# One weight sum of every seven-product unit moved from VectorE to GpSimd, in a two-layer decoder trunk

## The chip, the cores and the metric

The kernel runs on one core of a Trainium2 chip. The metric is the device time of one execution in microseconds (us). All matrices are float32, held as pairs of a rounded part and a rest.

## The reference

Two layers, each with a half-step feed-forward network (FFN) before and after a mixer; layer 0 mixes with retention, layer 1 with gated linear attention (GLA). 16 learned tokens are put ahead of the 512, so 528 tokens with 1024 features run through:

```
for i in range(2):
    h = h + 0.5 * swiglu(rmsnorm(h, norm_ffn1[i]), ffn1_w_in[i], ffn1_w_out[i])   # 1024 -> 2 x 2816 -> 1024
    hn = rmsnorm(h, norm_mix[i])
    h = h + (retention(hn, ...) if i == 0 else gla(hn, ...))
    h = h + 0.5 * swiglu(rmsnorm(h, norm_ffn2[i]), ffn2_w_in[i], ffn2_w_out[i])
h = rmsnorm(h, final_norm)
return h[:, 16:]
```

Nearly all of the time goes into the projections: the input and output matrices of the four FFNs (called f10, f20, f11, f21 in tile names, in the order f10, retention, f20, f11, GLA, f21) and of the two mixers.

## The kernel before

**Units of seven products.** Most weight matrices are used in units: two blocks of 128 weight columns against 528 tokens in two halves of 264, done by the Strassen-Winograd scheme with seven block products in place of eight. A unit's weight has the quarters a11, a12, a21, a22, each 128 rows by 512 (384 in the middle group of an FFN's output matrix). The products need four sums of them as well: s1 from a22 and a21, s3 from a11 and a21, s2 from s1 and a11, s4 from a12 and s2. `Weights.order` gives the order of the seven: UNIT (a11, s1, s2, a12, s4, s3, a22), LAST (s3 and s4 swapped), PARTED (a11, s1, a12, s2, ...), and FIRST (s1, s2, a12, a11, ...). PARTED is used in the first output unit of the last group of f10, f20 and f11; FIRST in the first unit of each FFN. Of the 150 units, 146 begin with a11 and 4 with s1.

**How a sum comes about.** SP loads a22 and a11 into a tile `pair` (two halves; L149), and then GpSimd issues one DMA that reads a21 and adds it to both (L155); after that the pair holds s1 and s3. There are three pair tiles, so a pair is loaded when the third unit before it has had its s3 or s1 split. Other quarters go into seven tiles `raw` (L158). VectorE makes s2 in the tile of a11 (L195: `raw<-pair,raw`) and later s4 in the tile of a12 (L197: `raw<-raw,raw`).

**Splitting.** `Weights._split` takes the plan's next weight: ScalarE rounds it into `whi` (L188), VectorE takes the rest into `wlo` (L189, weight minus `whi`). Seven pairs of those tiles are in the pool; the splits run some items ahead of the products (AHEAD = 4). A product is three matmuls per 128 x 128 block: hi with hi (L488), rest of the tokens (L489), rest of the weight (L490).

**Results.** A unit has a PSUM bank X, used several times, and a double bank QZ. ScalarE copies products out of X and Z (L727, L729, L734 to the tiles `su`, `szf` and others), and VectorE adds them (L1035, L998, L1070, L1077 among others). The next product that goes to X waits for that copy or addition, so these are the places where TensorE can come to wait for the two.

**What sets the order.** A scheduler puts each engine's instructions into one fixed order when the program is built; each engine then takes its own in that order and waits at the head of its queue for the semaphores of what it needs. That holds for the DMA issues too: an L155 on GpSimd's queue waits until its two SP loads have landed, and what stands behind it on that queue waits with it.

Of the kernel before, what the change touches and what calls it, by code (L numbers as in the profile page):

```python
# [68 lines left out]
class Weights:  # L69
# [92 lines left out]
    def _split(self, upto):  # L162
        V = self.nc.vector
        while self.split < min(upto, len(self.plan)):
            i = self.split
            home = next(((pool, there) for pool, n, there in self.homes if len(there) < n), None)
            if not home:
                break
            home[1].add(i)
            _, c, q, n, order = self.plan[i]  # L170
            self._load()
            if order:

                late = order[0] == "s1"
                s2 = self.tiles[c][:, 1] if late else self.tiles[c, "a11"]
                raw = {"s1": self.tiles[c][:, 1], "s3": self.tiles[c][:, 0], "s2": s2,
                       "s4": self.tiles[c, "a12"]}.get(q)
            if not order or raw is None:
                raw = self.tiles[c, q]
            hi = home[0].tile([P, PW], F32R, tag="hi", name=f"whi{i}")  # L180
            lo = home[0].tile([P, PW], F32R, tag="lo", name=f"wlo{i}")
            with ExitStack() as order_:
                if self.behind and i < self.FRONT:
                    for ins in self.behind:
                        order_.enter_context(self.tc.issue_after(ins.ins))
                if self.after:
                    order_.enter_context(self.tc.issue_after(self.after.ins))
                act = self.nc.scalar.copy(hi[:, :n], raw)  # L188
                dve = V.tensor_sub(lo[:, :n], raw, hi[:, :n].bitcast(F32))  # L189
                self.newest = act, dve  # L190
            self.parts[i] = (hi, lo)
            self.split += 1
            if order:
                if q == ("s1" if late else "a11"):
                    V.tensor_add(s2, self.tiles[c][:, 1], self.tiles[c, "a11"])  # L195
                elif q == "a12":
                    V.tensor_add(raw, raw, s2)  # L197
                self.over["pair"] += q == "s3"
                self.over["raw"] += q in self.OVER[2 if order == self.PARTED else late]
            else:  # L200
                self.over["raw"] += 1
            self._load()
# [2146 lines left out]
```

## Time and profile before

| | |
|---|---|
| median of 3 runs (lowest, highest) | 2019.59 us (2019.57, 2020.69) |
| profiled execution | 2020.17 us, of which the span of instructions 2018.4 us |
| TensorE busy | 1998.6 us, 99% of the span |
| VectorE busy | 1793.7 us, 89% |
| ScalarE busy | 1190.6 us, 59% |
| GpSimd busy | 209.8 us, 10%, in 181 instructions |
| granted TensorE clock | 0.999 |

All times in rows are microseconds from the start of the span. In a timeline row stand start, duration, engine (PE TensorE, DVE VectorE, ACT ScalarE, POOL GpSimd, SP the load queue), the line of the kernel, the operation with output and inputs, and in brackets the idle time before it with what ended it. TensorE's matmuls overlap in the rows (each is listed with 0.28 us and the next starts 0.12 us later), so its busy time says that it was never long without work, not more. A DVE row of 0.69 us starts some 0.60 us before the next when both stand back to back.

### The profile page before, as it was taken

To read this page: it belongs to the slowest core of one execution; us is meant where nothing else is said; L and a number is where in the kernel's file an instruction comes from. 1 tells how busy PE (TensorE), PEld (TensorE's weight loads), DVE (VectorE), ACT (ScalarE), POOL (GpSimd) and SP (SyncE) were. 2 spreads that over 40 slices of the span, in tenths; PEclk is the share of its full clock that TensorE was granted. 3 is DMA by queue.
4 is the path that set the end of the run, shared out by engine and by line. 5 is a ranking of instruction groups with operands and counts; after the bars stand their busy time and mean duration, and the time that the engine had idled before them with its cause. 6 is when DMAs were issued, how large, how long until landed. Compare 5 with 4: busy or idle time off the path is not lost.

```text
span 2018.4 us, 43487 instructions
## 1 busy us (share of the span) xinstructions
PE 1998.6 (99%) x16576; PEld 1964.3 (97%) x16576; DVE 1793.7 (89%) x3302; ACT 1190.6 (59%) x2427; POOL 209.8 (10%) x181
## 2 busy tenths in 40 slices
PE   9999999999999999999999999999999999999998
PEld 9999999999999999999999999999999989999998
DVE  8999999978787889989999998999897868999896
ACT  5756566555555465656666665666745544666664
POOL 1011111010101000111111011111001000211110
PEclk9999999999999999999999999999999999999999
DMA  7586877364545432776875477777525441687772
GB/s 228 138 208 168 205 194 188 101 163 121 157 132 147 132 116 74 181 202 161 213 186 163 128 189 187 180 199 181 183 69 126 105 137 65 159 208 182 185 191 69
DMA packets 176113, 318.87 MB, mean 158 GB/s; under 512 B 17568, under 2 KB 40736, under 8 KB 175904
## 3 DMA queue, kind: packets, MB, share of 16 engines
q1 hardware_dynamic: 133856, 237.04, 35.8%
q0 software_dynamic: 40896, 75.51, 23.4%
q10 hardware_dynamic: 1152, 3.55, 0.6%
q8 instruction: 130, 2.13, 0.4%
q14 instruction: 79, 0.65, 0.1%
HBM read 311.76 MB, written 4.26 MB: 157 GB/s over the span
## 4 chain that ended last, share of the span: by engine, by line
PE 83%; DVE 12%; ACT 2%; issue 2%; DMA 1%; POOL 0%; POOLq 0%; DVEq 0%; ACTq 0%
DVE wlo L189 4%; PE po_r L488 1%; PE po_r L489 1%; PE po_r L490 1%; PE lv L1866 1%; ACT whi L188 1%; DVE hf L521 1%; PE Xf21o L488 1%; PE Xf21o L490 1%; PE Xf21o L489 1%; PE Xf20u L488 1%; PE Xf11u L488 1%; PE Xf20u L490 1%; PE Xf11u L490 1%; PE Xf11u L489 1%
## 5 line engine op out<-in xcount | busy, mean ns | idle before, releaser
L188 ACT CAST whi<-raw 128x512 fp32r<-128x512 f32 (+1 forms) x893 | 531.9, 606 | 424.6 <-DVE raw L197 145.9
L189 DVE TENSOR_TENSOR wlo<-raw,whi 128x512 fp32r<-128x512 f32 (+1 forms) x893 | 590.3, 669 | 104.6 <-ACT whi L188 91.4
L188 ACT CAST whi<-pair 128x512 fp32r<-128x512 f32 (+1 forms) x304 | 183.4, 604 | 75.1 <-DVE pair L195 12.4
L189 DVE TENSOR_TENSOR wlo<-pair,whi 128x512 fp32r<-128x512 f32 (+1 forms) x304 | 201.8, 665 | 11.7 <-ACT whi L188 10.6
L155 POOL DMA_DIRECT2D pair<-in_f_in x73 | 89.0, 1220 | 704.6 <-DVE wlo L189 348.0
L197 DVE TENSOR_TENSOR raw<-raw,raw 128x512 f32<-128x512 f32 (+1 forms) x146 | 97.5, 668 | 3.6
L195 DVE TENSOR_TENSOR raw<-pair,raw 128x512 f32<-128x512 f32 (+1 forms) x146 | 97.2, 666 | 3.4 <-DMA pair<-in_f_in 0.8
L155 POOL DMA_DIRECT2D pair<-in_f_out x44 | 53.5, 1216 | 358.3 <-DVE wlo L189 122.8
L488 PE MATMUL po_r<-ogh,whi 128*128 128x264 f32 x256 | 71.7, 280 | 0.1
L489 PE MATMUL po_r<-ogl,whi 128*128 128x264 f32 x256 | 71.5, 279 | 0.0
L490 PE MATMUL po_r<-ogh,wlo 128*128 128x264 f32 x256 | 71.2, 278 | 0.0
L155 POOL DMA_DIRECT2D pair<-in_ret_in x20 | 24.4, 1222 | 308.6 <-DVE wlo L189 156.3
L999 ACT ACTIVATE gf<-gf 128x528 f32<-128x528 f32 (+1 forms) x36 | 23.2, 644 | 50.4 <-DVE gf L998 50.3
L488 PE MATMUL Xf11o<-hf,whi 128*128 128x264 f32 x176 | 49.5, 281 | 1.4 <-ACT szf L734 0.4
L488 PE MATMUL Xf20o<-hf,whi 128*128 128x264 f32 x176 | 49.5, 281 | 1.4 <-DVE x L1077 0.6
L488 PE MATMUL Xf10o<-hf,whi 128*128 128x264 f32 x176 | 49.5, 281 | 1.0 <-ACT szf L734 0.4
L489 PE MATMUL Xf11o<-hf,whi 128*128 128x264 f32 x176 | 49.1, 279 | 0.0
L489 PE MATMUL Xf20o<-hf,whi 128*128 128x264 f32 x176 | 49.1, 279 | 0.0
L489 PE MATMUL Xf10o<-hf,whi 128*128 128x264 f32 x176 | 49.1, 279 | 0.0
L488 PEld LDWEIGHTS po_r<-ogh,whi 128*128 128x128 f32 x256 | 48.0, 188 | 0.9 <-ACT k L521 0.3
L490 PE MATMUL Xf20o<-hf,wlo 128*128 128x264 f32 x176 | 48.9, 279 | 0.0
L490 PE MATMUL Xf10o<-hf,wlo 128*128 128x264 f32 x176 | 48.9, 279 | 0.0
(1183 smaller groups left out, 8598.8 us busy)
## 6 DMA issues: line engine op xcount, KB each, us to landing
raw<-in_f_in SPq DMA_DIRECT2D x277, 256.0 KB, 3.7
pair<-in_f_in SPq DMA_DIRECT2D x150, 256.0 KB, 5.0
pair<-in_f_in POOLq DMA_DIRECT2D x73, 512.0 KB, 7.4
raw<-in_f_out SPq DMA_DIRECT2D x80, 256.0 KB, 3.3
raw<-in_ret_in SPq DMA_DIRECT2D x76, 256.0 KB, 3.0
raw<-in_f_out SPq DMA_DIRECT2D x72, 192.0 KB, 3.0
pair<-in_f_out SPq DMA_DIRECT2D x48, 256.0 KB, 4.9
pair<-in_f_out POOLq DMA_DIRECT2D x24, 512.0 KB, 6.1
```

What stands on the lines that cost most here:

```text
L155: nc.gpsimd.dma_start(t, aps[2].unsqueeze(1).broadcast_to([P, 2, n]), accum_op=ALU.add)
L188: act = self.nc.scalar.copy(hi[:, :n], raw)
L189: dve = V.tensor_sub(lo[:, :n], raw, hi[:, :n].bitcast(F32))
L195: V.tensor_add(s2, self.tiles[c][:, 1], self.tiles[c, "a11"])
L197: V.tensor_add(raw, raw, s2)
L488: nc.tensor.matmul(ps, lhsT=lh, rhs=rh, start=start, stop=False, **kw)
L489: nc.tensor.matmul(ps, lhsT=lh, rhs=rl, start=False, stop=False, **kw)
L490: return nc.tensor.matmul(ps, lhsT=ll, rhs=rh, start=False, stop=stop, **kw)
L521: return S.copy(hi, src), V.tensor_sub(lo, src, hi.bitcast(F32))
L999: S.activation(o, o, AF.Silu, scale=-1.0)
L1866: nc.tensor.matmul(ps[:, j, J * P:J * P + n], lhsT=Kt[:, j, J * P:(J + 1) * P], rhs=q, start=(J == 0), stop=(J == 3), skip_group_check=True)
```

## The change

In units that begin with a11, the instruction L195, s2 = s1 + a11, is issued on GpSimd in place of VectorE. In the four units that begin with s1 it stays. s4 and all splits stay where they are.

```
             if order:
                 if q == ("s1" if late else "a11"):
-                    V.tensor_add(s2, self.tiles[c][:, 1], self.tiles[c, "a11"])
+                    (V if late else self.nc.gpsimd).tensor_add(s2, self.tiles[c][:, 1], self.tiles[c, "a11"])
                 elif q == "a12":
                     V.tensor_add(raw, raw, s2)
```

The scheduler then places 146 additions on GpSimd's queue between its DMA issues. On GpSimd, at the end of f10, the difference reads as follows (numbers behind a name count buffers: `pair36` and `raw94` belong to the first output unit of the last group, a PARTED one, and `pair38` to the second unit behind it):

```order
 L155 DMA pair36_4010<-in_f1_out 128x2x512
+L195 TENSOR_TENSOR raw91_3930<-pair35_3863,raw91_3930 128x512
 L155 DMA pair37_4148<-in_f1_out 128x2x512
 L155 DMA pair38_4276<-in_f1_out 128x2x512
+L195 TENSOR_TENSOR raw94_4065<-pair36_4010,raw94_4065 128x512
 L155 DMA pair39_4455<-in_f1_out 128x2x512
```

The sum of unit 36 stands behind the accumulating DMA of unit 38, that of unit 37 (not shown) behind the DMA of unit 39. On VectorE the same place reads as follows:

```order
+L197 TENSOR_TENSOR raw92_3972<-raw92_3972,raw91_3930 128x512
 L189 TENSOR_TENSOR wlo195_4273<-pair35_3863,whi195_4272 128x512
 L1003 TENSOR_TENSOR gf1021_4089<-Xf10g20_4090,su3_4092 128x264
-L197 TENSOR_TENSOR raw92_3972<-raw92_3972,raw91_3930 128x512
 L189 TENSOR_TENSOR wlo196_4294<-raw92_3972,whi196_4293 128x512
 L189 TENSOR_TENSOR wlo197_4313<-raw93_3991,whi197_4312 128x512
 L189 TENSOR_TENSOR wlo198_4332<-raw94_4065,whi198_4331 128x512
-L195 TENSOR_TENSOR raw94_4065<-pair36_4010,raw94_4065 128x512
 L189 TENSOR_TENSOR wlo199_4349<-pair36_4010,whi199_4348 128x512
 L189 TENSOR_TENSOR wlo200_4368<-raw95_4110,whi200_4367 128x512
```

Two things moved: L197 of the unit before now stands ahead of `wlo195`, the split that frees the pair tile for `pair38`; and the addition leaves the queue with nothing in its place. L197 of this unit (`raw95<-raw95,raw94`), L189 of `raw94` and then L1035 still follow in that order, and L197 now waits for GpSimd. On ScalarE, in retention, the rows around the split of a sum are these in the program of the change, the same as before but for what the second row waits for (`raw200` is the sum, made on GpSimd behind the DMA of `pair90`):

```order
L1432 COPY vt31_9470<-Xrv30_9471 128x264
L188 CAST whi394_9710<-raw200_9304 128x512
L734 COPY su5_9588<-Xrv32_9586 128x264
L188 CAST whi395_9727<-raw201_9428 128x512
L188 CAST whi396_9962<-pair78_9140 128x512
```

The copy L734 out of the bank `Xrv32`, behind it on the queue, moves with the cast.

More of the change, by code (lines that the diff above doesn't have):

```diff
@@ L194, in _split @@
                 if q == ("s1" if late else "a11"):
-                    V.tensor_add(s2, self.tiles[c][:, 1], self.tiles[c, "a11"])
+                    (V if late else self.nc.gpsimd).tensor_add(s2, self.tiles[c][:, 1], self.tiles[c, "a11"])
                 elif q == "a12":
```

## The prediction

> **What bounds the kernel now.** I read the page's shares first, then busy time by stretch, then the chain of waits, then single places in the timeline.
>
> ```profile
> PE 1998.6 (99%) x16576; PEld 1964.3 (97%) x16576; DVE 1793.7 (89%) x3302; ACT 1190.6 (59%) x2427; POOL 209.8 (10%) x181
> PE 83%; DVE 12%; ACT 2%; issue 2%; DMA 1%; POOL 0%; POOLq 0%; DVEq 0%; ACTq 0%
> ...
> L195 DVE TENSOR_TENSOR raw<-pair,raw 128x512 f32<-128x512 f32 (+1 forms) x146 | 97.2, 666 | 3.4 <-DMA pair<-in_f_in 0.8 <-DVE wlo L189 0.6
> ...
> 205.00:300.00 95.00, 95.00 (x813) 94.97 (x812) 87.81 (x158) 60.56 (x128) 13.39 (x11) 1.00 0.81 204
> 1050.00:1130.00 80.00, 78.79 (x658) 77.36 (x657) 76.52 (x140) 48.50 (x94) 6.79 (x6) 1.00 0.50 136
> ```
>
> The reader sees a kernel bound by TensorE: of 2018.4 us it lacks work for 19.8, and inside an FFN (205 to 300 us) for none, while VectorE there is at 87.81 of 95 us (92%). Only where one stage hands over to the next (1050 to 1130 us) is VectorE at 96% and TensorE short of work by 1.2 us. So 97.2 us of VectorE's work can go away and save almost nothing; what counts is whether something that TensorE waits for comes later. The chain's 12% of VectorE says where it is close. In the chain's pieces in order of time the instruction that moves appears ten times, the first and the last being
>
> ```profile
> 72.56 0.69 DVE raw L195
> ...
> 1784.94 0.70 DVE raw L195
> ```
>
> **What the change removes.** 146 additions of 0.666 us leave VectorE: 97.2 us of its busy time. On the path lie ten of them, 6.8 us at most, and that only if nothing takes their place. Inside the FFNs TensorE hides them, and would hide them still.
>
> **What the change adds: the price of a sum on GpSimd.** No row shows a GpSimd addition of 512 columns. The nearest rows are its small power operations, in the table of GpSimd's groups and in two stretches of the timeline:
>
> ```profile
> L462 POOL TENSOR_TENSOR rc<-ms_n,rc 128x1 f32<-128x1 f32 x4 | 2.2, 549 | 0.0
> ...
> 1535.82 1.03 POOL L462 TENSOR_TENSOR r_go<-ms_go,rc 128x4 f32<-128x4 f32 x1 [3.91 <-DVE ms_go L541]
> ...
> 1520.99 0.69 DVE L189 TENSOR_TENSOR wlo<-raw,whi 128x512 fp32r<-128x512 f32 x1
> 1521.16 1.40 POOL L462 TENSOR_TENSOR r_go<-ms_go,rc 128x4 f32<-128x4 f32 x1 [7.68 <-DVE ms_go L541]
> ```
>
> One column takes 0.55 us and four take 1.03, so a column of powers costs 0.16 and the fixed part is 0.55 - 0.16 = 0.39. The same four columns took 1.40 us when VectorE was 0.17 us into a subtraction of two SBUF tiles: 0.37 more. The streaming of 512 columns I take from VectorE, whose back-to-back rows start 0.61 us apart (296.86 and 297.47 below). My estimate is 0.39 + 0.61 + 0.37 = 1.37 us. The floor is 0.55 (the one-column operation); the top is 0.39 + 2 x 0.67 + 0.61 = 2.34, for half VectorE's rate behind a whole VectorE instruction. I take 1.37 because VectorE is at work nearly always, as in the 1.40 row. [...]
>
> **Where the price is hidden.** Most sums are free to start early: GpSimd's last DMA issue is long over, and the cast that reads the sum is late for other reasons. A unit in f10:
>
> ```profile
> 245.28 1.21 POOL L155 DMA_DIRECT2D pair<-in_f_in  x1 [7.00 <-DVE su L1036]
> 246.97 0.69 DVE L195 TENSOR_TENSOR raw<-pair,raw 128x512 f32<-128x512 f32 x1
> 250.22 1.14 ACT L188 CAST whi<-raw 128x512 fp32r<-128x512 f32 x2
> ```
>
> GpSimd is free at 246.49, the sum could end at 248.3, and its cast came at 250.22. With 1.37 us and each sum put behind its predecessor on the new queue, 130 of the 146 delay nothing that TensorE waits for by more than 0.05 us.
>
> **Where it is not hidden.** In 30 units the DMA issue that now stands ahead of the sum ended after the sum had begun on VectorE. That DMA can't come sooner: it waits for two loads, and these for the last split of an earlier pair. I list three kinds.
>
> First, the PARTED unit at the end of f10, f20 and f11, where L197 needs the sum almost at once:
>
> ```profile
> 296.86 0.69 DVE L195 TENSOR_TENSOR raw<-pair,raw 128x512 f32<-128x512 f32 x1
> 297.47 0.69 DVE L189 TENSOR_TENSOR wlo<-pair,whi 128x512 fp32r<-128x512 f32 x1
> 298.31 1.21 POOL L155 DMA_DIRECT2D pair<-in_f_out  x1 [6.62 <-DVE wlo L189]
> 298.84 0.69 DVE L197 TENSOR_TENSOR raw<-raw,raw 128x512 f32<-128x512 f32 x1
> 300.33 0.43 DVE L1035 TENSOR_TENSOR su<-Xf10u,su 128x264 f32<-128x264 f32 x1
> 301.53 0.28 PE L488 MATMUL Xf10u<-thf,whi 128*128 128x264 f32 x1
> ...
> 1044.76 0.69 DVE L197 TENSOR_TENSOR raw<-raw,raw 128x512 f32<-128x512 f32 x1
> 1045.43 1.22 POOL L155 DMA_DIRECT2D pair<-in_f_out  x1 [7.25 <-DMA pair<-in_f_out]
> ...
> 1380.10 0.69 DVE L197 TENSOR_TENSOR raw<-raw,raw 128x512 f32<-128x512 f32 x1
> 1380.58 1.22 POOL L155 DMA_DIRECT2D pair<-in_f_out  x1 [6.92 <-DVE wlo L189]
> ```
>
> At 297 us the DMA ends at 299.52, the sum at 300.89, and L197 starts 2.05 us later than at 298.84. L197 and one split at 0.61 each ended at 300.06, so VectorE had 0.27 us to spare before L1035; the matmul at 301.53, which needs L1035, had 0.77 (301.53 - 300.76). TensorE waits 2.05 - 0.27 - 0.77 = 1.0 us. The same at 1044.76 (DMA ends 1046.65, L197 3.26 late) gives 2.2, at 1380.10 (1381.80, 3.07 late) 2.0: together 5.2. The order adds 0.6 to each, since L197 of the unit before now stands ahead of the split that frees the pair: 1.8 more.
>
> Second, the unit after each of these. Here ScalarE stands still: the cast waits for the sum, and the copy out of X is queued behind the cast.
>
> ```profile
> 308.80 1.22 POOL L155 DMA_DIRECT2D pair<-in_f_out  x1 [9.27 <-DVE x L1076]
> 309.50 0.62 ACT L188 CAST whi<-raw 128x512 fp32r<-128x512 f32 x1 [0.33 <-DVE raw L195]
> 310.02 0.37 ACT L734 COPY szf<-Xf10o 128x264 f32<-128x264 f32 x1
> 310.94 0.28 PE L488 MATMUL Xf10o<-hf,whi 128*128 128x264 f32 x1
> ```
>
> The sum would end at 310.02 + 1.37 = 311.39, the cast start 1.9 us late, the copy with it; the matmul had 0.55 to spare: 1.4. In the other two FFNs the picture is the same: 4.2 in all.
>
> Third, retention and GLA, with the same queue on ScalarE and less to spare:
>
> ```profile
> 487.22 1.22 POOL L155 DMA_DIRECT2D pair<-in_ret_in  x1 [8.34 <-DVE raw L195]
> 487.47 0.62 ACT L188 CAST whi<-raw 128x512 fp32r<-128x512 f32 x1 [0.95 <-PE Xrv L489]
> 489.40 0.37 ACT L734 COPY su<-Xrv 128x264 f32<-128x264 f32 x1
> 490.14 0.28 PE L488 MATMUL Xrv<-rth,whi 128*128 128x264 f32 x1
> ...
> 689.08 0.62 ACT L188 CAST whi<-raw 128x512 fp32r<-128x512 f32 x1 [0.50 <-DVE wlo L189]
> 689.32 1.22 POOL L155 DMA_DIRECT2D pair<-in_f_in  x1 [7.88 <-DVE wlo L189]
> 689.60 0.37 ACT L734 COPY su<-Xrv 128x264 f32<-128x264 f32 x1
> 690.35 0.28 PE L488 MATMUL Xrv<-rth,whi 128*128 128x264 f32 x1
> ```
>
> At 689 us the sum ends at 691.91, the cast is 2.83 late, and the matmul after the copy had 0.38: 2.45. At 487 us the cast is 2.34 late, 0.5 of that is made up before the copy, and 0.37 is to spare: 1.4. Four more places, at 413, 495, 613 and 1546 us, are worth 2.4 by the same steps. Inside the FFNs (229, 1310, 1785 and 1862 us) there are 1.5.
>
> **The sum.** 5.2 + 1.8 + 4.2 + 2.45 + 1.4 + 2.4 + 1.5 = 19 us. Against it stands what VectorE gains on the path, between 0 and 6.8; I take 2, since eight of the ten pieces lie at hand-overs that now wait for the sum. That is 2020.2 + 17 = 2037 us. The profiled execution lies 0.6 above the median shown; I leave that in. With a sum of 0.55 us the same places give 7, with 2.34 some 43.
>
> **Rivals.** *Half of it* (2027): a wait hides a later one, for once TensorE stands still at 301.5 everything that it needs next has been given that much more time. For this speaks that the second kind follows the first by 10 us; against it, that the DMA of the second kind is itself freed by VectorE, which is late too. It holds if the cast of the second kind is no later against TensorE than before: 19 - 4.2 - 1.8 - 2 = 11, less what ScalarE makes up in retention, leaves 7.
>
> *VectorE held up* (2050): GpSimd's read stops VectorE's two-input instructions for its whole length, as the 1.40 row shows the other way round. Then each sum costs VectorE up to 1.37 - 0.39 = 0.98 us in place of 0.61; net 146 x 0.37 = 54 us, and at the 20 or so units near hand-overs, where VectorE is as full as at 1050 to 1130 us, it goes straight on: 7 us, and the waits of the sum grow by about as much, as more of the sums come late. Against it: inside the FFNs 7 us in 95 are free. [...]
>
> *Faster* (2014): GpSimd's DMA issue is not in the way, for instance since loads go out sooner with a freer VectorE, and the ten additions on the chain are saved: 6.8 less. It decides if the sum at 297 us ends before 298.84, so the loads would have to land 2 us sooner; they are freed by a split that TensorE paces, which speaks against it.
>
> *No change* (2016 to 2024): the waits are eaten by idle times that I have counted too small, and 4 us are left of either sign.
>
> **The numbers.** Main case 0.52 (2029 to 2045), half of it 0.16, VectorE held up 0.17, no change 0.09, faster 0.06. A measurement of this kernel tells 0.2% (4 us) from no change. Faster: 0.06. Same: 0.09. Slower: 0.52 + 0.16 + 0.17 = 0.85. The range 2022 to 2052 leaves out the faster case, half of no change and a part of held up, 0.18 in all.
>
> **What the profile after would show.** VectorE at about 1700 us if it is not held up, at 1800 or more if it is, with rows of L189 well over 0.69. GpSimd's L195 at 1.2 to 1.6 us. New waits of VectorE L197 and ScalarE L188 for POOL L195, in total tens of us, and of TensorE 1 to 3 us each at the three hand-overs and in retention. I am wrong if L155 is no longer ahead of the sum in time at 297 us, or if these waits are there and TensorE's are not.

## The result, and the profile after

The changed kernel takes 2078.68 us (2077.83 to 2086.15, four runs) against 2019.58 us (2019.52 to 2020.69, four runs): 1.030 times as long, 95% interval 1.028 to 1.032. The forecast was 2037 with a range to 2052. The sign was right, the size less than a third of what came. The profiled execution took 2079.27 us, its span 2077.3.

The page of the changed kernel, busy time by engine, the chain of waits and three groups of instructions (busy us, mean ns, idle time before them):

```profile
PE 2022.4 (97%) x16576; PEld 1980.7 (95%) x16576; DVE 1824.3 (88%) x3156; ACT 1191.0 (57%) x2427; POOL 458.0 (22%) x327
...
PE 65%; DVE 18%; DMA 6%; issue 4%; ACT 3%; POOL 2%; SPq 0%; DVEq 0%; ACTq 0%; POOLq 0%
...
L189 DVE TENSOR_TENSOR wlo<-raw,whi 128x512 fp32r<-128x512 f32 (+1 forms) x893 | 637.6, 725 | 100.9 <-ACT whi L188 77.8
L195 POOL TENSOR_TENSOR raw<-pair,raw 128x512 f32<-128x512 f32 (+1 forms) x146 | 258.0, 1767 | 685.3 <-DVE wlo L189 685.2
L189 DVE TENSOR_TENSOR wlo<-pair,whi 128x512 fp32r<-128x512 f32 (+1 forms) x304 | 245.7, 808 | 28.4 <-ACT whi L188 23.3
```

In the chain TensorE's share fell from 83% to 65%; VectorE has 18% (12% before), transfers 6% (1%). The first line tells most: VectorE has 146 instructions fewer and is busy 30.6 us longer (1793.7 before). The rows of the additions sum to 97.2 us, but back-to-back rows overlap: with no sums at all VectorE is busy for 1715.3 us (first experiment below). So 78.4 us went away, and 109.0 (1824.3 - 1715.3) came back inside other instructions. The split L189 has the same instructions and work as before, and takes 725 and 808 ns on average where it took 669 and 665; of its 1197 rows 107 are now longer than 0.8 us, up to 2.95, and before none was. The addition itself takes 1.77 us on GpSimd, 1.86 at 512 columns.

One place shows how. The timeline inside f10, rows of GpSimd and VectorE at two sums (start, duration, engine, line):

```profile
252.66 0.43 DVE L667 SCALAR_TENSOR_TENSOR t1f10h<-su,t0f10h 128x264 f32<-128x264 f32 x1
252.83 2.63 POOL L195 TENSOR_TENSOR raw<-pair,raw 128x512 f32<-128x512 f32 x1 [0.49 <-DVE wlo L189]
...
253.00 0.68 DVE L189 TENSOR_TENSOR wlo<-pair,whi 128x512 fp32r<-128x512 f32 x1
253.60 0.70 DVE L521 TENSOR_TENSOR hf<-t0f10h,hf 128x528 fp32r<-128x528 f32 x1
254.22 0.43 DVE L1042 SCALAR_TENSOR_TENSOR su<-Xf10u,gf 128x264 f32<-128x264 f32 x1
254.56 1.45 DVE L189 TENSOR_TENSOR wlo<-raw,whi 128x512 fp32r<-128x512 f32 x1
...
263.21 0.69 DVE L189 TENSOR_TENSOR wlo<-pair,whi 128x512 fp32r<-128x512 f32 x1
263.28 1.76 POOL L195 TENSOR_TENSOR raw<-pair,raw 128x512 f32<-128x512 f32 x1 [2.86 <-DVE wlo L189]
...
264.01 1.58 DVE L189 TENSOR_TENSOR wlo<-raw,whi 128x512 fp32r<-128x512 f32 x1
```

At 263.28 the addition starts while VectorE is in a subtraction of two SBUF tiles. The next subtraction starts at 264.01 and lasts till 265.59, 0.55 us (one such instruction's work) after the addition's end at 265.04: it stood still until GpSimd was done. At 252.83 the order is turned round: VectorE runs three two-input instructions without a gap, and only at 254.22, with L1042, of whose inputs one is in PSUM, does GpSimd seem to come in. It ends at 255.46, 1.24 us later, about the length of the shortest additions of 512 columns (1.26 to 1.28), and the split of 254.56 again ends 0.55 us behind it. So each side waits for the other in turn.

By stretch, inside f10, at the end of f20 with the start of f11, and two short ones (columns: us, busy PE, PEld, VectorE, ScalarE, GpSimd, granted clock, DMA share, GB/s); the first two are shifted with the kernel:

```profile
211.00:306.00 95.00, 94.95 (x806) 94.39 (x805) 88.73 (x144) 59.48 (x127) 29.63 (x20) 1.00 0.78 200
1084.00:1164.00 80.00, 74.51 (x610) 72.42 (x610) 75.25 (x133) 44.51 (x86) 11.08 (x9) 1.00 0.53 138
310.10:316.90 6.80, 5.37 (x24) 5.37 (x25) 6.46 (x14) 3.64 (x8) 0.00 (x0) 0.50 0.86 220
419.40:426.20 6.80, 6.80 (x37) 6.78 (x36) 4.78 (x13) 3.40 (x11) 0.00 (x0) 0.50 0.24 59
```

Inside the FFN TensorE still lacks nothing, with VectorE at 88.73 of 95. At the end of f20 and the start of f11 (1084 to 1164) it now lacks 5.5 us. The last two rows are new: stretches at half TensorE clock. There are four in the changed kernel (6.83 us at 310, 3.41 at 365, 6.83 at 419, 6.83 at 1433); the kernel before has one alone, at its very end. 23.9 us at half clock cost up to 12.

The waits of the changed kernel (in total, times, longest):

```profile
ACT whi L188 <- POOL raw L195: 107.5, 70, 5.0
DVE raw L197 <- POOL raw L195: 11.1, 3, 4.5
...
PE Xf10u L488 <- DVE su L1035: 5.6, 3, 3.4
...
PE Xf11u L488 <- DVE su L1035: 4.1, 2, 2.8
PE Xrv L488 <- ACT su L734: 3.1, 2, 2.1
```

The forecast's waits are there: L197 three times, at the three PARTED units, and ScalarE's casts. So is TensorE behind L1035. The first of the three places, in the timeline by engine:

```profile
307.25 1.21 POOL L155 DMA_DIRECT2D pair<-in_f_out  x1 [8.51 <-DMA pair<-in_f_out]
308.00 1.75 POOL L195 TENSOR_TENSOR raw<-pair,raw 128x512 f32<-128x512 f32 x1
...
309.79 0.69 DVE L197 TENSOR_TENSOR raw<-raw,raw 128x512 f32<-128x512 f32 x1 [4.54 <-POOL raw L195]
...
309.79 0.62 ACT L188 CAST whi<-raw 128x512 fp32r<-128x512 f32 x1 [4.99 <-POOL raw L195]
...
311.53 0.59 PE L488 MATMUL Xf10u<-thf,whi 128*128 128x264 f32 x1 [3.39 <-DVE su L1035]
```

The matmul at 311.53 lasts 0.59 us and not 0.28: the clock dropped to half at 310.1, during the stall.

### The profile page after: what moved, and what is told of

Same layout as the page of the kernel before. It is cut to its first block, busy times and chain, and to the rows that moved or that the text cites. A ratio compares the mean times of both kernels' runs of the same rounds, so it can differ in the third digit from the quotient of the medians.

```text
span 2077.3 us, 43628 instructions
## 1 busy us (share of the span) xinstructions
PE 2022.4 (97%) x16576; PEld 1980.7 (95%) x16576; DVE 1824.3 (88%) x3156; ACT 1191.0 (57%) x2427; POOL 458.0 (22%) x327
## 4 chain that ended last, share of the span: by engine, by line
PE 65%; DVE 18%; DMA 6%; issue 4%; ACT 3%; POOL 2%; SPq 0%; DVEq 0%; ACTq 0%; POOLq 0%
DVE wlo L189 6%; DMA pair<-in_f_in 2%; DMA pair<-in_f_out 2%; ACT whi L188 2%; POOL raw L195 2%; DVE raw L197 1%; DVE hf L521 1%; PE lv L1866 1%; PE po_r L488 1%; PE po_r L489 1%; PE po_r L490 1%; PE Xf21u L488 1%; PE Xf21u L489 1%; PE Xf21u L490 1%; PE Xf21g L488 1%
## 5 line engine op out<-in xcount | busy, mean ns | idle before, releaser
L189 DVE TENSOR_TENSOR wlo<-raw,whi 128x512 fp32r<-128x512 f32 (+1 forms) x893 | 637.6, 725 | 100.9 <-ACT whi L188 77.8
L195 POOL TENSOR_TENSOR raw<-pair,raw 128x512 f32<-128x512 f32 (+1 forms) x146 | 258.0, 1767 | 685.3 <-DVE wlo L189 685.2
L189 DVE TENSOR_TENSOR wlo<-pair,whi 128x512 fp32r<-128x512 f32 (+1 forms) x304 | 245.7, 808 | 28.4 <-ACT whi L188 23.3
L197 DVE TENSOR_TENSOR raw<-raw,raw 128x512 f32<-128x512 f32 (+1 forms) x146 | 97.2, 666 | 14.1 <-POOL raw L195 11.1
L521 ACT CAST hf<-su 128x792 fp32r<-128x792 f32 (+4 forms) x41 | 31.7, 782 | 32.6 <-DVE su L1042 32.0
L489 PE MATMUL Xf10o<-hf,whi 128*128 128x264 f32 x176 | 49.6, 282 | 0.0
L490 PE MATMUL Xf11o<-hf,wlo 128*128 128x264 f32 x176 | 49.3, 281 | 0.0
```

The lines of the kernel that those rows point to most:

```text
L195: (V if late else self.nc.gpsimd).tensor_add(s2, self.tiles[c][:, 1], self.tiles[c, "a11"])
L489: nc.tensor.matmul(ps, lhsT=lh, rhs=rl, start=False, stop=False, **kw)
L490: return nc.tensor.matmul(ps, lhsT=ll, rhs=rh, start=False, stop=stop, **kw)
L521: return S.copy(hi, src), V.tensor_sub(lo, src, hi.bitcast(F32))
```

## The experiments

All have the same matmuls, so the start of a matmul can be compared with that of the same matmul in the kernel before. The table gives what each kernel loses (+) or gains (-) in four kinds of stretches, summed from those starts, in us of the profiled executions. FFN starts are 0 to 150, 760 to 900, 1080 to 1200 and 1660 to 1830 us after the first matmul of the kernel before; FFN ends with the mixer's or next FFN's first matmuls 290 to 400, 1040 to 1080 and 1340 to 1450; mixers 400 to 760 and 1450 to 1660; the rest is inside the FFNs. In some kernels a few matmuls change places, so single entries are good to some tenths.

```
                                  FFN starts  inside  ends  mixers  total
the change                            13.9      6.2   26.8   12.1    59.0
no sums                               -8.2      0.1   -0.9   -0.2    -9.2
GpSimd memset, not read               -9.9     -0.1   -1.2   -0.2   -11.4
GpSimd copy, not read                 -5.5     -0.1    4.9    0.0    -0.7
GpSimd addition, not read              8.9      4.0   18.8    5.1    36.8
three GpSimd memsets, read            -3.3      1.8   16.5    9.4    24.4
sums ahead of the DMAs                15.1      6.0   14.8   16.1    51.9
only the three PARTED                 -1.2      0.2   10.4    0.3     9.7
all but the three PARTED              14.5      5.9   18.1   12.0    50.5
88 units inside the FFNs               6.3      5.6    0.3    0.6    12.8
15 sums by DMA at FFN starts          -7.3      0.4    0.1    0.3    -6.4
```

Three theories stood against each other: the queue (a sum stands late behind a DMA issue on GpSimd), the lock (GpSimd's reading holds VectorE), and the half clock, which would multiply either.

**No sums.** What VectorE's relief is worth alone.

```
+                    if late:
                         V.tensor_add(s2, self.tiles[c][:, 1], self.tiles[c, "a11"])
-                s2 = self.tiles[c][:, 1] if late else self.tiles[c, "a11"]
+                s2 = self.tiles[c][:, 1]
```

> The 146 sums are left out altogether (s1 is used in the place of s2, so the output is another); all else as before. It gives the worth of VectorE's relief alone. VectorE's busy time falls by 97 us to about 1697. All theories agree on little: TensorE is without work for 20 us, ten sums on the chain are 6.8 us at most, so 2013 to 2019 us. If it comes to 2005 or less, VectorE's load counted for more than the chain showed.

2011.15 us (ratio 0.9954, 0.9938 to 0.9971), 8.6 less than before and more than any theory gave it. The table puts nearly all of it at the FFN starts. VectorE is busy for 1715.3 us, not the 1697 expected: 78.4 less than before.

**The addition, with no reader.** As above, and in place of the sum

```
+                    self.nc.gpsimd.tensor_add(self.tiles[c, "a11"], self.tiles[c][:, 1], self.tiles[c, "a11"])
```

> As the run without sums, but GpSimd still does the 146 additions, on the same tiles in the same place of its queue; nothing reads what they write. So it has the contention of the change without its dependency. Queue theory (the changed kernel's 59 us come from sums that end late, behind an accumulating DMA): within 4 us of the run without sums, 2013 to 2022. Lock theory (a VectorE instruction with two SBUF inputs stands still while GpSimd reads, and GpSimd waits in turn while VectorE runs such instructions without a gap): VectorE's L189 has again 60 or more rows above 0.8 us, 100 to 130 us held in all, and about half of the 59 us stays: 2035 to 2050.

2056.78 us (1.0175, 1.0153 to 1.0196). No split waits for the sum, and still it is 46 us more than without it. Only the next load into the tile waits, and that is no cause: ScalarE and VectorE wait 5.6 us in all for loads of raw tiles, 6.9 in the next kernel. The queue theory's 2013 to 2022 is out. Two stretches at half clock, 3.41 us at 359 and 6.83 at 411, cost up to 5 of the 46.

**A memset in its place, with no reader.**

```
+                    self.nc.gpsimd.memset(self.tiles[c, "a11"], 0.0)
```

> As the run in which nothing reads GpSimd's additions (2056.8 us), but in the place of each addition stands a GpSimd memset of the same tile: it writes the same 512 columns and reads nothing. VectorE, ScalarE and TensorE have the same instructions in the same order as there and as in the run without sums (2011.2 us). Lock theory (GpSimd's reading of two SBUF tiles is what holds VectorE): L189 has no row above 0.8 us, and the time is that without sums, 2009 to 2015. If an instruction more on GpSimd's queue, the later DMA issue behind it, or its writing is what costs, most of the 46 us between the two stays: 2035 or more.

2009.42 us (0.9951, 0.9935 to 0.9968). VectorE, ScalarE and TensorE have the same instructions in the same order in both kernels, and GpSimd's queue has one instruction in the same place; it reads two tiles in the one and nothing in the other. VectorE's splits of raw tiles in a query by line (min, median, max in ns), first with the addition:

```profile
L189 DVE TENSOR_TENSOR wlo<-raw,whi x747: 541/685/2660, 5.6 to 2027.7; 128x512 fp32r<-128x512 f32 x163, 128x384 fp32r<-128x384 f32 x24
```

and with the memset:

```profile
L189 DVE TENSOR_TENSOR wlo<-raw,whi x747: 547/685/729, 5.7 to 1979.4; 128x512 fp32r<-128x512 f32 x163, 128x384 fp32r<-128x384 f32 x24
```

The median is the same, the maximum 2660 against 729 ns. The pages' busy lines, addition and then memset, each from its own kernel:

```profile
PE 2012.3 (98%) x16576; PEld 1972.8 (96%) x16576; DVE 1830.6 (89%) x3156; ACT 1191.6 (58%) x2427; POOL 457.3 (22%) x327
```

```profile
PE 1991.6 (99%) x16576; PEld 1961.7 (98%) x16576; DVE 1715.1 (85%) x3156; ACT 1195.2 (60%) x2427; POOL 283.3 (14%) x327
```

VectorE is held for 1830.6 - 1715.1 = 115.5 us, 0.79 us per sum, and 47.4 us of it reach the end (2056.78 - 2009.42). So the reading is the cause, and neither the queue slot nor the write. One difference is left, since the memset is shorter (0.60 us against 1.85 at 512 columns); the kernel with three memsets, below, settles it.

**A copy in its place, with no reader.**

```
+                    self.nc.gpsimd.tensor_copy(self.tiles[c, "a11"], self.tiles[c][:, 1])
```

> The same with a GpSimd copy of s1 into the tile: one tile read in place of two. Lock theory, if any read of SBUF takes the lock: VectorE held about in proportion to the copy's length, which with one input should be 0.6 to 1.3 us against 1.75; 2025 to 2050. If only two-input instructions of GpSimd take it: 2009 to 2016.

2020.33 us (1.0004, 0.9995 to 1.0013), between the two forecasts. A query by line of the copy:

```profile
L198 POOL COPY raw<-pair x146: 501/1013/4068, 60.9 to 1966.9; 128x512 f32<-128x512 f32 x122, 128x384 f32<-128x384 f32 x24
```

VectorE's busy time is 1737.3 us, so it is held for 22 us (1715.1 with the memset), a fifth of what the addition takes, and the loss is 11. One input is enough, then, but it costs far less than half. The copy's shortest row is 0.50 us, half the addition's (1.00; both of 384 columns); why the hold shrinks five times and not two was not settled.

**Three memsets, read.** The dependency without the reading.

```
-                    V.tensor_add(s2, self.tiles[c][:, 1], self.tiles[c, "a11"])
+                    for _ in range(3):
+                        self.nc.gpsimd.memset(s2, 0.0)
```

> The changed kernel with three GpSimd memsets of the tile in the place of each addition (3 x 0.52 = 1.56 us against 1.77): they wait for the split of a11 and stand in GpSimd's queue like the addition, the cast of s2 and VectorE's s4 wait for them, and they read nothing (the weight is zero, so the output is another). So it has the dependency and the queue of the change without its reading of SBUF; the scheduler puts some instructions in another order, so it is no exact counterpart. If the two costs add up (memset that nobody reads 2009.4, plus 22 us that readers added to the free addition): 2028 to 2036. If the queue costs only because VectorE is held as well: 2010 to 2020. If the queue is most of the 59 us after all: 2050 or more.

2044.67 us (1.0121, 1.0106 to 1.0136), 35 over the memset that nobody reads, where 19 to 27 was expected. GpSimd's memsets take 237 us in all, near the additions' 257, and yet VectorE is busy for 1713.8 us and no split is stretched:

```profile
L189 DVE TENSOR_TENSOR wlo<-raw,whi x893: 544/685/726, 5.5 to 2015.2; 128x512 fp32r<-128x512 f32 x155, 128x384 fp32r<-128x384 f32 x24
```

So the length of GpSimd's work does not hold VectorE; its reading does. TensorE's longest waits:

```profile
PE Xf20u L492 <- DVE su L1039: 6.1, 2, 6.0
PE Xf11u L492 <- DVE su L1039: 3.9, 1, 3.9
PE Xrv L492 <- DVE vt L1433: 2.6, 1, 2.6
```

They are the PARTED units of f20 and f11 and retention, places that the forecast named; with the first two go 6.83 us each at half clock. The FFN starts lose nothing here (-3.3 in the table). The scheduler gave some instructions another order, so the 35 is no exact part of the change. The two causes do not add: the addition without readers loses 47 over its memset, the readers without the addition's reads 35, both together 69 (2078.68 - 2009.42).

**Only the three PARTED units.**

```
+                    (self.nc.gpsimd if order == self.PARTED else V).tensor_add(s2, ...)
```

> Only the three PARTED units' sums are on GpSimd, 143 stay on VectorE. Queue theory with TensorE's clock: three stalls of 1.7 to 3.6 us (8 us in all), each of about 3 us followed by 6.8 us at half clock, which loses 3.4 us; two or three such stretches: 2034 to 2040. Queue theory without the clock: 2027 to 2029. Lock theory: three instructions hold VectorE for 4 us at most: 2020 to 2024.

2029.33 us (1.0045, 1.0030 to 1.0060): 9.5 us from three instructions. By the starts of the matmuls TensorE stands still for 2.0, 2.8 and 2.5 us at the three places, 7.3 in all; after the first and third follow 3.41 us at half clock. The first wait, and the first stretch:

```profile
303.77 0.39 PE L488 MATMUL Xf10u<-thf,whi 128*128 128x264 f32 x1 [1.83 <-DVE su L1035]
```

```profile
305.30:308.70 3.40, 3.40 (x18) 3.40 (x17) 3.40 (x8) 2.33 (x5) 0.00 (x0) 0.50 0.82 246
```

At half clock each stretch loses up to 1.7 us, so up to 3.4 of the 9.5 are the clock's. Without the clock 2027 to 2029 was expected, with it 2034 to 2040; it is the upper edge of the first, with smaller stalls and shorter stretches than in the whole change.

**All but the three PARTED units.**

```
+                    (V if late or order == self.PARTED else self.nc.gpsimd).tensor_add(s2, ...)
```

> The changed kernel with the sums of the three PARTED units back on VectorE. Queue theory with these three as the main thing: their own cost alone was 9.7 us, so 2067 to 2070 if it adds up, and less, 2060 to 2066, if the half-clock stretches at 310 and 1433 us also go with them. Lock theory agrees that the rest, 45 to 50 us, stays.

2073.21 us (1.0269, 1.0254 to 1.0285). That is 5.5 us less than the change by the medians and 8.5 by the profiled executions; the four runs of each kernel spread by 7 and 8 us, so whether the 9.7 add up is not shown. The two 6.83 us stretches at half clock that followed PARTED units are gone, and so is the one of 3.41 at 365; one of 3.41 came at 321 us. It follows a stall at the unit after the PARTED one (ScalarE, then TensorE):

```profile
319.02 0.62 ACT L188 CAST whi<-raw 128x512 fp32r<-128x512 f32 x1 [2.84 <-POOL raw L195]
319.55 0.37 ACT L734 COPY szf<-Xf10o 128x264 f32<-128x264 f32 x1
319.97 0.39 PE L488 MATMUL Xf10o<-hf,whi 128*128 128x264 f32 x1 [1.88 <-ACT szf L734]
```

This is the forecast's second kind, cast, copy and matmul. By the starts of the matmuls TensorE loses 2.0, 1.9 and 1.3 us at these units of f10, f20 and f11, 5.3 in all (4.2 forecast). In the changed kernel it loses 0.5 us there in f20 and nothing to speak of in the others: the stall at the PARTED unit comes first and hides it.

**The sum ahead of the DMA.** The accumulating DMA of a pair is kept back and queued behind the next unit's sum:

```
-                        nc.gpsimd.dma_start(t, aps[2]..., accum_op=ALU.add)
+                        self.due.append((c, t, aps[2]...))
...
+                    ins = self.nc.gpsimd.tensor_add(s2, self.tiles[c][:, 1], self.tiles[c, "a11"])
+                    with self.tc.issue_after(ins.ins):
+                        for _, t, a21 in self.due:
+                            self.nc.gpsimd.dma_start(t, a21, accum_op=ALU.add)
+                    self.due = []
```

> The changed kernel with one difference: each accumulating DMA of a pair is queued on GpSimd behind the next unit's sum in place of ahead of it, so that no sum waits for the DMA's loads. Queue theory: the stalls at the three PARTED units and in retention go, and with them the half clock: 2020 to 2035. Lock theory: VectorE is held as in the changed kernel, 20 us at most of the 59 go: 2058 to 2075.

2072.07 us (1.0255, 1.0240 to 1.0270). The FFN ends go from 26.8 to 14.8, so 12 us are taken away where the queue was the cause; the mixers lose 4 more. There, a DMA that came behind one sum now stands ahead of a later one (timeline, GpSimd and then ScalarE):

```profile
715.43 1.22 POOL L165 DMA_DIRECT2D pair<-in_f_in  x1 [7.74 <-DMA raw<-in_ret_in]
716.18 1.76 POOL L203 TENSOR_TENSOR raw<-pair,raw 128x512 f32<-128x512 f32 x1
...
717.98 0.62 ACT L196 CAST whi<-raw 128x512 fp32r<-128x512 f32 x1 [6.22 <-POOL raw L203]
```

with a wait of TensorE of 5.2 us behind ScalarE's copy, and 6.83 us at half clock. The other 52 us stay, within what the lock theory had (2058 to 2075), the new stall in the mixers among them.

**Only inside the FFNs.**

```
+ inside = key[2] == "i" and key[4] >= 8 or key[2] == "o" and key[3] < 2
+ (self.nc.gpsimd if inside and not late else V).tensor_add(s2, ...)
```

> GpSimd makes the sums of only those 89 units that lie inside the FFNs: the units of the input matrices from the second group on and the output units of the first two groups. The other 57, near the FFNs' starts and ends and in the mixers, stay on VectorE. Theory that place decides (VectorE is held everywhere alike, but inside an FFN TensorE covers it): 61% of the sums cost a tenth of the 59 us: 2021 to 2028. If each sum costs the same wherever it stands: 59 x 89/146 = 36, so 2050 to 2060. If what VectorE loses inside an FFN is carried on to its end, 2030 to 2045, with the time lost at 296 to 350, 1040 to 1080 and 1340 to 1400 us of the kernel before.

2034.47 us (1.0072, 1.0057 to 1.0087). Its sums on GpSimd:

```profile
L196 POOL TENSOR_TENSOR raw<-pair,raw 128x512 f32<-128x512 f32 (+1 forms) x88 | 155.2, 1764 | 229.7 <-DVE wlo L189 229.6
```

88 sums are on GpSimd, and VectorE is busy for 1816.2 us: 22.5 more than before. The rows that left it sum to 88 x 0.666 = 58.6, but by the run without sums only 78.4 x 88/146 = 47.3 of VectorE's busy time, so it is held for some 70 us. The time is some 14 us longer. By the same working the other 58 sums of the change hold VectorE for 109 - 70 = 39 us and, with their own lateness, cost 59 - 14 = 45. So place decides, but less sharply than 2021 to 2028 said: the 14 are a fifth of the hold, about half of them in the table's FFN starts, where the second groups of the input matrices begin, and inside an FFN TensorE is not quite covered.

**The sum by a DMA.** Two ways of relieving VectorE with no operand read on GpSimd: an accumulating DMA from the pair into a11's tile,

```
-                    V.tensor_add(s2, self.tiles[c][:, 1], self.tiles[c, "a11"])
+                    self.nc.gpsimd.dma_start(s2, self.tiles[c][:, 1], accum_op=ALU.add)
```

> The sum made by an accumulating DMA from the pair tile into the tile of a11, issued by GpSimd, in place of an addition by any engine. VectorE is relieved of 97 us and nothing on GpSimd reads SBUF as an operand. Lock theory: no L189 row above 0.8 us. But the DMA takes 1.2 us to issue and 5 us to land, against 0.67 for the addition, and a cast that has some 3 us of room after the sum would be late by 3 us in many units: 2030 to 2200, with the waits of ScalarE L188 for a DMA into raw. If the splits run far enough ahead it is 2011 to 2019 and better than the kernel before.

2337.34 us (1.158, 1.156 to 1.160): the cast waits for it.

```profile
ACT whi L188 <- DMA raw<-pair: 442.8, 127, 8.4
```

And into a second copy of a11, loaded ahead (`for q in ("a11", "s2", "a12", "a22")` in the loads of the raw tiles, the DMA as soon as pair and copy have been asked for):

> No engine adds: a11 is loaded a second time into a raw tile of its own, and an accumulating DMA from the pair tile makes s2 there as soon as both have landed, well ahead of the split. It costs 146 loads of 256 KB more on SP, 146 DMA issues of 0.95 us on GpSimd, and a fourth of the seven raw tiles for each unit. If that is in time nearly everywhere, VectorE's relief comes out as in the runs without sums: 2008 to 2014 us, faster than before. If seven raw tiles are too few for four loads per unit, or the DMA engines (at 0.5 to 0.8 of their time before) fill up, loads come late and TensorE waits: 2030 to 2100.

2147.64 us (1.0625, 1.0594 to 1.0656). Seven raw tiles are too few: the DMA waits for a tile to come free (`wlo` by VectorE), and the cast waits for the DMA.

```profile
POOL raw L164 <- DVE wlo L194: 368.3, 41, 22.2
...
ACT whi L193 <- DMA raw<-pair: 166.0, 52, 6.4
```

But at some FFN starts this kernel kept the relief: 2.0 us at 1140 to 1200 and 1.3 at 1700 to 1740, by the starts of the matmuls. Hence the last one, with the second copy only in the input units of the first group:

```
+        twice = order not in (self.FIRST, self.PARTED) and key[2:3] == ("i",) and key[4] < 8
+        for q in ("a11", "s2", "a12", "a22") if twice else ("a11", "a12", "a22"):
```

> The kernel before, with the sum made by an accumulating DMA into a second copy of a11 in only those 15 units that begin the FFNs (input units of the first group), where the run without sums gained 1.0, 2.4, 2.4 and 1.6 us and the run with all sums by DMA lost little. If VectorE's load is what counts there and the DMA is in time: 2011 to 2016, faster than before. If the fourth raw tile or the DMA makes loads late there: 2018 to 2030.

2014.80 us (0.9975, 0.9965 to 0.9985): faster than the kernel before by some 5 us, and so than both. The start of f20 in the kernel before, and then in this one:

```profile
820.00:872.00 52.00, 51.12 (x428) 50.32 (x427) 50.34 (x89) 33.55 (x67) 7.07 (x6) 1.00 0.72 185
```

```profile
820.00:872.00 52.00, 51.67 (x441) 51.47 (x441) 49.50 (x87) 34.06 (x69) 7.27 (x6) 1.00 0.77 199
```

In the same 52 us TensorE does 441 matmuls in place of 428. The matmuls that begin in this stretch before take 51.9 us there and 50.3 here.

## Why the prediction was wrong

**The step that failed: the sum has no term for VectorE being held.** The main case prices only when each sum ends and who waits for it, and lets VectorE run on undisturbed, with a gain of 2 us. The hold stands in a rival alone, *VectorE held up*, with 0.17, and that rival is the larger cause: the kernels whose GpSimd reads two tiles and whose GpSimd only writes one, with everything else in the same order, are 47.4 us apart, and three memsets of nearly the additions' length in all do not hold VectorE. Even the rival's 2050 is 29 us short. Its hold was not too small: it took 0.98 us per sum against the 0.61 that left VectorE, net 54 us, and measured are 0.79 per sum with no reader (115.5/146) and 0.75 in the change (109/146) against 0.54, net 31 in the change. What failed in it is the step from VectorE to TensorE, "at the 20 or so units near hand-overs ... 7 us". In the kernel whose sums nobody reads VectorE is busy 36.9 us longer than before, and the time is 37 us longer. Of the 115.5 us held, 47.4 came through; by the table (48.2 in the profiled executions) at the FFN starts 18.8 (8.9 + 9.9), at the ends 20.0, in the mixers 5.3 and inside 4.1.

**VectorE's gain was too small as well.** I took 2 us of at most 6.8, from ten pieces of the chain. That list held only the 195 longest pieces. The whole chain has 17 pieces of the sum, 9.7 us (those at 825.31 and 1715.12, of 0.60 each, were missing among others). Without the sums the kernel is 8.6 us faster, so 6.8 was no upper bound. By place even the whole chain does not foretell it: 4.1 of its 9.7 us lie at the FFN starts, where 8.2 were gained. There VectorE is at 97% (50.34 of 52 us at 820 to 872, quoted above), and the 425 matmuls that begin in that stretch take 51.9 us, against 49.6 without the sums. Where relief is worth 8 us, a hold costs too: 18.8 us at the same places.

**"130 of the 146 delay nothing" was an argument about the sum, not about VectorE.** For the sum's own lateness it is about right: inside the FFNs the readers add 2.2 us (6.2 - 4.0) to what the lock takes, against 1.5 forecast. At the FFN starts, where the forecast had nothing, they add 5.0 (13.9 - 8.9). And the 88 sums inside cost 14 us in all, VectorE's hold included.

**The queue was there, at the places named, and larger than 19 us.** The three PARTED units were to cost 7.0; alone they cost 9.5, of which 7.3 are stalls. The second kind, ScalarE behind the cast in the unit after, was to cost 4.2; it costs 5.3 where the PARTED unit does not stall (VectorE's hold may add to it), and at most 0.5 at one place in the changed kernel. So the step of the rival *half of it*, that a wait hides a later one, holds here, and the sum counted both. In retention 1.4 and 2.45 us were forecast, and by the starts of the changed kernel's matmuls TensorE lost 1.14 and 2.26 there. With readers and without the lock, but in another order, the waits cost 35 us (2044.67 - 2009.42), up to 7 of them half clock; on top of the lock they cost 22. That this kernel lies only 24 us above the kernel before, not far from the 17 forecast, is partly luck: a larger cost and a larger relief cancel. I also let GpSimd's price be one number: 1.37 us is near the 1.28 of the shortest additions, and the mean at 512 columns is 1.86, within the ends that I gave.

**The half clock was missing.** No term of the sum had it: each stall was priced at its own length. Up to 12 of the 59 us lie in it.

So of 59: about -10 for the relief, +47 for the hold, and +22 for the readers on top (2078.68 - 2056.78), the half clock being part of the last two. What I said the profile would show did tell the two apart: VectorE "at 1800 or more" with L189 "well over 0.69" is what came, at 1824.3 and up to 2.95.

## What to carry to other kernels

A two-input addition on GpSimd was not free here beside a VectorE that runs two-input instructions on SBUF: 78 us of VectorE's time went away and 109 came back. Before moving work, leave it out altogether in one run and let the new engine do it with no reader in another; here these two gave the gain (8.6 us) and the hold's price (46), and the pieces that I had counted on the chain gave neither. A DMA relieved VectorE without that price, and what decided here was whether it was in time: in 15 units at the FFN starts, issued ahead, it gained 5 us with the splits of raw tiles at a mean of 670 ns (669 before), and in all 146 the casts waited 443 us for it, 166 with the second copy.

## What the hardware showed that I had not expected

GpSimd's wait was not for one VectorE instruction: at 252.83 it lasted through three in a row, and the longest addition took 4.12 us in the changed kernel, against 1.26 for the shortest of 512 columns. Then VectorE was held for the rest of the addition: the split of 254.56 took 1.45 us, where the one of 253.00 took 0.68.

TensorE's clock fell to half for 3.41 or 6.83 us with stalls that were shorter than that: in the kernel with three sums 2.0 us, ended at 303.77, was enough, while 2.8 us at 1051 in the same kernel had no such stretch behind it. The half-clock stretches stand at even distances: in the changed kernel those at 365, 419 and 1433 begin 54.6, 109.2 and 1123.0 us after the one at 310, which is 16, 32 and 329 times 3.413, and the two of the kernel with three sums begin 1088.85 us apart, 319 times 3.413. Counted in such steps, the one ahead of the first stretch of that kernel, and the two over which its stall of 2.8 us falls:

```profile
301.88:305.29 3.41, 1.58 (x13) 1.52 (x13) 3.26 (x7) 1.76 (x3) 0.12 (x1) 1.00 0.99 187
1049.40:1052.81 3.41, 2.29 (x20) 2.08 (x18) 0.22 (x1) 0.22 (x1) 2.52 (x2) 1.00 0.42 84
1052.81:1056.22 3.41, 1.89 (x15) 1.89 (x16) 3.41 (x7) 1.76 (x4) 0.00 (x0) 1.00 0.98 208
```

TensorE was idle for 0.54 of the first, and for 0.33 and 0.45 of the other two. So the length of a stall alone does not tell what came of it here; where it fell in these steps counted too. In the changed kernel, from 201 to 2016 us, TensorE was idle for 0.58, 0.74 and 0.60 of the steps ahead of the stretches at 310, 419 and 1433, and for 0.41 at most of any step at full clock that had no half-clock stretch behind it. The step ahead of the one at 365 was idle for only 0.34; that is not explained.
